# Two hybrid decoder layers on one core: values of two heads in one projection, the indexer's key beside the values, the rope key behind the first query tile, and another order of the sparse attention's first steps

## Chip, core and metric

The kernel runs on one core of a Trainium2 chip. The metric is the device time of one execution in microseconds; of several executions the median counts. The engines are PE (TensorE, matmuls), DVE (VectorE), ACT (ScalarE), POOL (GpSimd) and SP (SyncE, which issues most DMAs).

## What is computed

Two decoder layers over 512 tokens of 1024 features, in fp32. Each layer is a token mixer, a cross-attention into 256 memory tokens and a SwiGLU feed-forward part, each followed by a residual LayerNorm. The first mixer is multi-head latent attention (MLA), the second a sparse attention with an indexer (DSA). Cut to what the change touches:

```
# MLA: one input projection gives cq (512), ckv (256) and the rope key (32)
h = x @ w_in
q  = rms_norm(h[..., :512]) @ w_uq;  kv = rms_norm(h[..., 512:768]) @ w_ukv
k_rope = apply_rope(h[..., 768:800], pos)          # one key for all heads
# cross-attention, 4 heads of 256
q = x @ w_q;  k, v = split(mem @ w_kv)
p = softmax(q k^T / 16);  y = (p v) @ w_o
# DSA: queries 1024, keys 256, values 256, indexer queries 512, key 64, weights 8
h = x @ w_in
score = sum_h w_idx_h * relu(q_idx_h . k_idx / 8)   # top 128 keys of each query stay
p = softmax(q k^T / 8 + bias[bucket(distance)] on the chosen keys);  y = (p v) @ w_o
```

## The kernel before

Every product in full precision is three matmuls (`mm3`, L121, records on L122, L123, L124): operands are split into a high part, rounded by a cast on ACT (L99), and a low part, the difference, made by DVE or POOL (L101); high by high, high by low and low by high are accumulated in PSUM. Weights come in chunks of 512 KB (`chunk`, L108: load by SP, L112, then the split), through three `raw` buffers and five each for high and low parts. Activations lie transposed, features on partitions, in tiles of 2 KB (`t2`, 39 of them) and 8 KB (`t8`, 9) per partition. PSUM has two groups of four banks, "a" and "b". A framework puts the instructions on the engines in an order by priority and dependences, close to the order of the code; an engine then runs its own list strictly in order.

**The beginning** (L167 to L573). x comes transposed in three loads on SP's queue and is split in four pieces. The compression of keys and values with the rope key, 304 columns (`w_ckv`), is loaded in four chunks of two k-blocks: three on ACT's queue, the fourth on SP's (L491) when a buffer is free. 96 matmuls of 304 columns fill four banks. Positions and constants for the angles are loaded after that (L508, L509); DVE computes the angles (`trig`, L449). For each of four token tiles the rope key is copied four times side by side by two ACT copies (L521), transposed by PE (L522), and copied to SBUF (L524). Then come the four chunks of `w_cq` and four query tiles of 24 matmuls of 512 columns; each tile's normalising (`rms_t`, L527: square on ACT, L530; DVE, L533; transposes, L536) is placed behind a later tile's matmuls.

**Cross-attention** (`xa_kv` L714, `cross` L733). Per head: scores, the next head's queries, its keys (48 matmuls of 256 columns, memory tokens moving) and its values (48 of 256 columns, weights moving, two chunks), then the softmax's normalising, its transposes (L766), and the product with the values.

**DSA projections** (L930 to L971). Values and the eight indexer weights are one projection, 264 columns moving, token tiles as stationary operand: 96 matmuls. The indexer's key, twice 64 features, is a feature tile of its own (`w_ki`): 24 matmuls of 512 columns. Four tiles of indexer queries follow, and scores for the top-k.

**DSA attention** (L1004 to L1121). 16 items (query tile, group of four heads), item = 4 x tile + group. Eight projections of queries run in a loop, DVE doing five top-k steps in each (L978, L979); the high parts of the queries are made by ACT, low parts by POOL (`stack_q_pool`, L927, L928). Between them, and after, stand the steps of the items: `s` (scores, L1026 to L1028, then scaling with the bias on DVE, L420), `t` (normalising and transposes, L1041, L1043), `p` (product with the values, L1060, L1061, L1071, and output copies on POOL, L1076, L1077). The order is written out:

```
steps = {2: "s0", 3: "t0", 4: "s1 p0", 5: "t1", 6: "s2 p1", 7: "t2"}   # after query projection j
run_s(3); run("p2"); run_s(4); run_t(3)     # then, for i = 3 to 15: scores ahead, t of the next, p of i
```

The bias of an item is read from a table in DRAM (`dsa_bias`, L1004, DMA at L1008): those of the first four items early, into `t2` tiles, the others with the scores, into `t8` tiles.

## Time and profile before

| | us |
|---|---|
| median of three timed runs | 1540.42 |
| lowest, highest | 1538.08, 1541.06 |
| the profiled execution's own time | 1538.13 |
| its span, first to last instruction | 1536.3 |
| PE busy | 1503.6 (98%) |
| DVE, ACT, POOL busy | 994.9, 650.2, 303.9 |
| mean granted clock of PE | 0.996 |

A row of a timeline is one instruction, or some alike in a row. A matmul's record spans from its start to its modelled end and overlaps its successor's, so that the price of one is read from the distance of two starts. Brackets give the time in which the engine had nothing running, and what it waited for.

### The profile page before, as it was taken

How to read it: one execution, taken by the hardware profiler on the slowest of the kernel's cores; microseconds unless marked ns; L12 is line 12 of the kernel's file. 1: busy time of each engine (PE TensorE's matmuls, PEld its weight loads, DVE VectorE, ACT ScalarE, POOL GpSimd, SP SyncE). 2: the span in 40 equal slices, each digit the busy share in tenths (PEclk: the TensorE clock that was granted, in tenths of full speed). 3: DMA queues.
4: the chain of work that ended last, by engine and by line, in shares of the span. 5: the costliest groups of instructions: out<-in, count | busy, mean ns of one | idle time of the engine just before them, and what ended most of it. 6: DMA issues, size and time to landing. Idle time of an engine off the chain costs nothing.

```text
span 1536.3 us, 20733 instructions
## 1 busy us (share of the span) xinstructions
PE 1503.6 (98%) x7902; PEld 1283.5 (84%) x7902; DVE 994.9 (65%) x1741; ACT 650.2 (42%) x1158; POOL 303.9 (20%) x299
## 2 busy tenths in 40 slices
PE   8999999999999999999999989999999999999997
PEld 7788889988898888888888787898988888888886
DVE  7787868454746665654668988675448465656545
ACT  5677753343233333332246577344332433333230
POOL 1222001000032331400024653000002322324002
PEclk9999999999999999999999999999999999999999
DMA  6233424323333232233242147333323233222221
GB/s 214 71 98 107 155 83 134 125 85 97 124 97 101 77 124 97 96 97 108 84 138 87 51 158 240 110 119 102 110 94 125 83 110 98 102 94 90 97 96 55
DMA packets 51417, 166.45 MB, mean 108 GB/s; under 512 B 5300, under 2 KB 11972, under 8 KB 49268
## 3 DMA queue, kind: packets, MB, share of 16 engines
q1 hardware_dynamic: 50740, 164.18, 32.6%
q8 instruction: 62, 1.02, 0.3%
q10 hardware_dynamic: 576, 0.93, 0.2%
q14 instruction: 39, 0.32, 0.1%
HBM read 160.86 MB, written 9.47 MB: 111 GB/s over the span
## 4 chain that ended last, share of the span: by engine, by line
PE 88%; DVE 5%; ACT 3%; DMA 2%; issue 1%; POOL 1%; SPq 0%; POOLq 0%; DVEq 0%; ACTq 0%
PE ps L122 27%; PE ps L123 27%; PE ps L124 27%; DVE t L101 2%; PE ps L336 1%; ACT wh L99 1%; ACT t L426 1%; ACT t L99 1%; DMA raw<-in_w_cq_dram 1%; PE ps L1043 1%; PE ps L644 1%; DMA t<-in_xT_dram 1%; PE ps L1060 0%; POOL wl L101 0%; DMA t<-scr 0%
## 5 line engine op out<-in xcount | busy, mean ns | idle before, releaser
L122 PE MATMUL ps<-t,wh 128*128 128x512 f32 (+1 forms) x1256 | 456.2, 364 | 3.5 <-DVE t L101 3.4
L123 PE MATMUL ps<-t,wh 128*128 128x512 f32 (+1 forms) x1256 | 455.2, 362 | 0.8 <-DVE t L101 0.8
L124 PE MATMUL ps<-t,wl 128*128 128x512 f32 (+1 forms) x1256 | 454.9, 362 | 0.0
L99 ACT CAST wh<-raw 128x1024 fp32r<-128x1024 f32 (+3 forms) x219 | 227.4, 1038 | 450.0 <-PE ps L123 167.1
L101 DVE TENSOR_TENSOR wl<-raw,wh 128x1024 fp32r<-128x1024 f32 (+2 forms) x198 | 253.2, 1280 | 218.0 <-ACT wh L99 216.3
L122 PE MATMUL ps<-wh,t 128*128 128x512 f32 (+3 forms) x838 | 305.4, 364 | 1.1 <-ACT t L426 0.9
L123 PE MATMUL ps<-wl,t 128*128 128x512 f32 (+3 forms) x838 | 303.1, 362 | 1.2 <-DVE wl L101 1.2
L124 PE MATMUL ps<-wh,t 128*128 128x512 f32 (+3 forms) x838 | 303.0, 362 | 0.2 <-DVE t L101 0.2
L122 PEld LDWEIGHTS ps<-t,wh 128*128 128x128 f32 x1256 | 237.1, 189 | 41.5 <-DVE t L101 5.5
L123 PEld LDWEIGHTS ps<-t,wh 128*128 128x128 f32 x1256 | 237.2, 189 | 37.0 <-DVE t L101 1.3
L124 PEld LDWEIGHTS ps<-t,wl 128*128 128x128 f32 x1256 | 237.1, 189 | 36.6
L122 PEld LDWEIGHTS ps<-wh,t 128*128 128x128 f32 x838 | 158.5, 189 | 25.1 <-ACT t L426 1.3
L123 PEld LDWEIGHTS ps<-wl,t 128*128 128x128 f32 x838 | 158.4, 189 | 24.6 <-DVE wl L101 1.4
L124 PEld LDWEIGHTS ps<-wh,t 128*128 128x128 f32 x838 | 158.4, 189 | 24.0 <-DVE t L101 0.4
L99 ACT CAST t<-ps 128x512 fp32r<-128x512 f32 (+2 forms) x249 | 122.9, 525 | 129.3 <-PE ps L336 86.1
L279 POOL TENSOR_TENSOR sm<-sm,mhalf 128x1 f32<-128x1 f32 x32 | 28.6, 893 | 689.0 <-DVE sm L277 689.0
L101 DVE TENSOR_TENSOR t<-ps,t 128x512 fp32r<-128x512 f32 (+2 forms) x249 | 144.1, 607 | 20.3 <-ACT t L99 19.5
L99 ACT CAST wh<-t 128x1024 fp32r<-128x1024 f32 x56 | 58.9, 1052 | 141.9 <-PE ps L123 123.6
L101 DVE TENSOR_TENSOR wl<-t,wh 128x1024 fp32r<-128x1024 f32 x56 | 71.2, 1272 | 65.2 <-ACT wh L99 63.4
L863 DVE TENSOR_TENSOR t<-ps,t 128x512 f32<-128x512 f32 x44 | 30.4, 692 | 120.1 <-PE ps L124 120.1
L101 DVE TENSOR_TENSOR t<-t,t 128x512 fp32r<-128x512 f32 (+2 forms) x113 | 84.5, 751 | 23.0 <-ACT t L99 20.7
L99 ACT CAST t<-t 128x512 fp32r<-128x512 f32 (+2 forms) x113 | 64.5, 574 | 56.2 <-POOL t L797 33.6
(178 smaller groups left out, 1654.5 us busy)
## 6 DMA issues: line engine op xcount, KB each, us to landing
raw<-in_ffn_in_dram SPq DMA_DIRECT2D x88, 512.0 KB, 3.5
t<-in_ffn_dg_dram SPq DMA_DIRECT2D x16, 1024.0 KB, 5.0
raw<-in_xa_k_dram SPq DMA_DIRECT2D x16, 512.0 KB, 3.5
raw<-in_xa_v_dram SPq DMA_DIRECT2D x16, 512.0 KB, 3.9
raw<-in_xa_q_dram SPq DMA_DIRECT2D x16, 512.0 KB, 3.9
raw<-in_xa_o_dram SPq DMA_DIRECT2D x16, 512.0 KB, 3.4
raw<-in_ffn_dl_dram SPq DMA_DIRECT2D x12, 512.0 KB, 3.4
scr<-vscr SPq DMA_DIRECT2D x16, 319.5 KB, 4.4
```

The source lines that it names most:

```text
L99: nc.scalar.copy(h, src)
L101: (eng or nc.vector).tensor_tensor(l, src, h.bitcast(F32), op=ALU.subtract)
L122: nc.tensor.matmul(ps, st[0], mv[0], start=start, stop=False, skip_group_check=more)
L123: nc.tensor.matmul(ps, st[0], mv[1], start=False, stop=False, skip_group_check=more)
L124: nc.tensor.matmul(ps, st[1], mv[0], start=False, stop=stop, skip_group_check=more)
L279: nc.gpsimd.tensor_tensor(b, a, mhalf, op=ALU.pow)
L336: nc.tensor.transpose(pt[:, k], x_of(tt)[:, 512 * n + P * k:512 * n + P * k + P], ident)
L426: nc.scalar.activation(Sx, src, AF.Exp, bias=nb, scale=scale, accum_out=self.sm[:, i:i + 1])
L644: nc.tensor.transpose(pt[:, P * qt:P * qt + P], Ss[qt][:, P * kb:P * kb + P], ident)
L863: nc.vector.tensor_tensor(sg, pu, sg, op=ALU.mult)
L1043: nc.tensor.transpose(pt[:, P * i:P * i + P], Ss[i][:, P * kb:P * kb + P], ident)
```

## The change

Five edits.

1. `w_ckv` is laid out with all k-blocks side by side and loaded in three tiles of three, three and two k-blocks (first tile in two pieces, of one and two k-blocks), all on ACT's queue; there is no fourth load on SP. Positions and constants stand behind x at the head of SP's queue.
2. The copies, transposes and last copy of the rope key become `rope_key()`, called after the first query tile and the normalising of the first key/value tile.
3. The values of heads 0 and 1, and of 2 and 3, are projected together: 48 matmuls of 512 columns ahead of an even head, from four chunks, and none ahead of an odd one. The transposes of a head's softmax (`turned`) stand before the next head's keys.
4. `w_ki` is gone; its 64 columns are the last of `w_vi`, 328 columns wide. Per token tile ACT copies them twice side by side, and PE transposes them into one bank.
5. The scores of item 0 come after the fourth query projection and not the third, and so on; behind the last projection the scores of items 4, 3 and 5 come before the product of item 2. The bias of item 4 is read early too, into two `t2` tiles by two DMAs.

The diff, cut to its core (the host's layout functions, which follow it, are left out):

```diff
-    def pairs_of(tile_):
-        return tile_[:, 0:2 * NC0].rearrange("p (k m) -> p k m", k=2)
-    raw_w = [pairs_of(wp.tile([P, 1024], F32, tag="raw", name=nm("raw"), bufs=3)) for _ in range(3)]
+    def threes(tag, dt, bufs=5):
+        ts = [wp.tile([P, 1024], dt, tag=tag, name=nm(tag), bufs=bufs) for _ in range(3)]
+        return [t[:, 0:3 * NC0].rearrange("p (k m) -> p k m", k=3) for t in ts]
+    raw_w = threes("raw", F32, 3)
...
-    wr = A["w_ckv"].rearrange("c p (k m) -> c p k m", k=2)
-    for i in range(2):
+    wr = A["w_ckv"].rearrange("p (k m) -> p k m", k=NK)
+    for i, ks in enumerate((slice(0, 1), slice(1, 3))):
         nc.sync.dma_start(raw_x[0][:, i], xr[0, :, i])
-        nc.scalar.dma_start(raw_w[0][:, i], wr[0, :, i])
+        nc.scalar.dma_start(raw_w[0][:, ks], wr[:, ks])
...
+    posi = t2(I32)
+    nc.sync.dma_start(posi, A["positions"].broadcast_to((P, S)))
+    nc.sync.dma_start(cst, A["consts"])
...
+    w_parts = {0: (0, 0, 1), 1: (0, 1, 3), 2: (1, 0, 3), 6: (2, 0, 2)}
...
-            sw = slice(i, i + step)
-            split(wh[:, sw], wl[:, sw], rw[:, sw])
+            if 2 * c + i in w_parts:
+                t, a, b = w_parts[2 * c + i]
+                split(whs[t][:, a:b], wls[t][:, a:b], raw_w[t][:, a:b])
...
-    pkb = bank("a")
-    for tt in range(NT):
-        kr = t2(F32, (P, 2, 2, 32))
-        for a in range(2):
-            c0 = 256 + 16 * a
-            nc.scalar.copy(kr[:, a], ps2[tt][:, c0:c0 + 32].unsqueeze(1).broadcast_to((P, 2, 32)))
-        nc.tensor.transpose(pkb[:, ts_of(tt)], kr.rearrange("p a b c -> p (a b c)"), ident)
     pk = t2()
-    nc.scalar.copy(pk, pkb)
+    def rope_key():
+        pkb = bank("a")
+        for tt in range(NT):
...
+        nc.scalar.copy(pk, pkb)
...
         rms_t(ps2[tt], 256, tt, gkv[:, 0:256], ckv)
         if tt:
             rms_t(psq[tt - 1], 512, tt - 1, gq, cq)
+        if tt == 0:
+            rope_key()
...
-        ws = [chunk(A["xa_v"][i, hd, c], (P, 4, 256)) for c in range(2)]
-        pv = bank("a", (P, 2, 256))
-        for mt in range(2):
-            for k in range(NK):
+        if hd % 2:
+            return Kt, None
+        ws = [chunk(A["xa_v"][i, hd // 2, c], (P, 2, 512)) for c in range(4)]
+        pvs = [bank("a") for _ in range(2)]
+        for k in range(NK):
+            w = ws[k // 2]
+            for mt in range(2):
                 ms = slice(P * mt, P * mt + P)
-                w = ws[k // 4]
-                mm3(pv[:, mt], (m[k][0][:, ms], m[k][1][:, ms]), (w[0][:, k % 4], w[1][:, k % 4]), k == 0, k == NK - 1)
+                mm3(pvs[mt], (m[k][0][:, ms], m[k][1][:, ms]), (w[0][:, k % 2], w[1][:, k % 2]), k == 0, k == NK - 1)
...
             Ss = scores(hd, Q)
             if hd < 3:
                 Q = q_proj(hd + 1)
+            PT = turned(Ss)
+            if hd < 3:
                 kvs[hd + 1] = xa_kv(i, hd + 1, m)
-            pv(hd, Ss)
+            pv(hd, PT)
...
+    pk = bank("b")
...
-            mm3(pv[:, 0:264], (xh[:, ts_], xl[:, ts_]), (w[0][:, k % 3], w[1][:, k % 3]), k == 0, k == NK - 1)
+            mm3(pv[:, 0:NV], (xh[:, ts_], xl[:, ts_]), (w[0][:, k % 3], w[1][:, k % 3]), k == 0, k == NK - 1)
...
-    (pk,) = proj_tiles([chunk(A["w_ki"], (P, NK, P))], XT, False)
+        ki = t2(F32, (P, 2, 64))
+        nc.scalar.copy(ki, pv[:, 264:NV].unsqueeze(1).broadcast_to((P, 2, 64)))
+        nc.tensor.transpose(pk[:, ts_], ki.rearrange("p a b -> p (a b)"), ident)
...
-        bt = t8(F32, (P, 4, 512)) if qt else t2(F32, (P, 4, P))
-        read = nc.sync.dma_start(bt[:, :, 0:n],
+        if (qt, g) == (1, 0):
+            bts = [t2(F32, (P, 2, 256)) for _ in range(2)]
+        else:
+            bts = [t8(F32, (P, 4, 512)) if qt else t2(F32, (P, 4, P))]
...
-        bt = dsa_bias(qt, g) if qt else first_bias[g]
+        bt = dsa_bias(qt, g) if 4 * qt + g > 4 else first_bias[4 * qt + g]
...
-    steps = {2: "s0", 3: "t0", 4: "s1 p0", 5: "t1", 6: "s2 p1", 7: "t2"}
+    steps = {3: "s0", 4: "t0 s1", 5: "p0 t1", 6: "s2 p1", 7: "t2"}
...
-        if j < 4:
-            first_bias.append(dsa_bias(0, j))
+        if j < 5:
+            first_bias.append(dsa_bias(j // 4, j % 4))
...
+    run_s(4)
     run_s(3)
+    run_s(5)
     run("p2")
-    run_s(4)
     run_t(3)
     for i in range(3, 16):
         a = 1 if i < LA else 0
         if i != LA:
-            run_s(i + 1 + a)
+            if i > 3:
+                run_s(i + 1 + a)
             run_t(i + a)
```

How it moves instructions, at two places. In the names, `ps` is a PSUM bank and the numbers tell buffers apart; the diff shifts line numbers (L99 becomes L100, L122 to L124 become L123 to L125, L522 becomes L528, L536 becomes L540, L1026 to L1028 become L1051 to L1053).

**The rope key, on ACT.** Before, from the third `w_cq` cast on: four-fold copies of the key (L521), the `w_v` cast, the copy back (L524), the first square (L530):

```order
L99 CAST wh_312<-raw_310 128x1024
L99 CAST wh_318<-raw_316 128x1024
L521 COPY t_37_280<-ps_127 128x64 x2
L521 COPY t_38_284<-ps_128 128x64 x2
L521 COPY t_39_288<-ps_129 128x64 x2
L521 COPY t_40_292<-ps_130 128x64 x2
L99 CAST wh_541<-raw_539 128x1024
L524 COPY t_41_296<-ps_279 128x512
L530 ACTIVATE t_55_347,sm_348<-ps_127 128x256
```

After:

```order
L100 CAST wh_288<-raw_286 128x1024
L100 CAST wh_294<-raw_292 128x1024
L534 ACTIVATE t_47_323,sm_324<-ps_130 128x256
L100 CAST wh_535<-raw_533 128x1024
L527 COPY t_54_338<-ps_130 128x64 x2
L527 COPY t_55_342<-ps_131 128x64 x2
L527 COPY t_56_346<-ps_132 128x64 x2
L527 COPY t_57_350<-ps_133 128x64 x2
L100 CAST t_12_122<-ps_332 128x2x128
L529 COPY t_33_273<-ps_337 128x512
```

The square of the first key/value tile (L534) and the `w_v` cast now stand ahead of the copies (L527), and the copies behind all four `w_cq` casts as before.

**The same place on PE.** Before: the last 304-column matmul, the transposes of the rope key (L522) among the first matmuls of the first query tile (`ps_322`), its end, and the first normalising's transposes (L536):

```order
L124 MATMUL ps_130<-wh_227,t_10_118 128x304
L522 MATMUL ps_279<-ident,t_37_280 128x128
L522 MATMUL ps_279<-ident,t_38_284 128x128
L522 MATMUL ps_279<-ident,t_39_288 128x128
L122 MATMUL ps_322<-wh_300,t_7_115 128x512
L522 MATMUL ps_279<-ident,t_40_292 128x128
L123 MATMUL ps_322<-wl_301,t_7_115 128x512
L124 MATMUL ps_322<-wh_300,t_8_116 128x512
...
L124 MATMUL ps_322<-wh_318,t_10_118 128x512
L536 MATMUL ps_356<-ident,t_59_354 128x128 x2
L122 MATMUL ps_367<-wh_300,t_7_115 128x512
```

After:

```order
L125 MATMUL ps_133<-wh_136,t_11_121 128x304
L123 MATMUL ps_298<-wh_276,t_8_118 128x512
L124 MATMUL ps_298<-wl_277,t_8_118 128x512
L125 MATMUL ps_298<-wh_276,t_9_119 128x512
...
L125 MATMUL ps_298<-wh_294,t_11_121 128x512
L540 MATMUL ps_332<-ident,t_51_330 128x128 x2
L528 MATMUL ps_337<-ident,t_54_338 128x128
L528 MATMUL ps_337<-ident,t_55_342 128x128
L528 MATMUL ps_337<-ident,t_56_346 128x128
L528 MATMUL ps_337<-ident,t_57_350 128x128
L123 MATMUL ps_361<-wh_276,t_8_118 128x512
```

The whole first query tile (`ps_298`) follows the last 304-column matmul; the transposes of the first key/value tile (L540) and of the rope key (L528) stand between it and the second tile.

**The end of the query projections, on PE.** Before: the last matmul of the eighth projection (`ps_11530`), item 2's transposes (L1041), item 3's scores (four pairs L1027, L1028; the last two use the last projection's queries) with item 2's remainder (L105, which subtracts the high part) among them:

```order
L124 MATMUL ps_11530<-t_1393_10106,wl_11527 128x512
L1041 MATMUL ps_11567<-ident,t_1578_11099 128x128 x4
L1027 MATMUL ps_11579<-t_1554_10981,t_1667_11459 128x256
L1028 MATMUL ps_11579<-t_1554_10981,t_1667_11459 128x256
L1027 MATMUL ps_11584<-t_1554_10981,t_1668_11460 128x256
L1028 MATMUL ps_11584<-t_1554_10981,t_1668_11460 128x256
L1027 MATMUL ps_11589<-t_1554_10981,t_1693_11555 128x256
L1028 MATMUL ps_11589<-t_1554_10981,t_1693_11555 128x256
L105 MATMUL ps_11567<-t_1699_11572,identn 128x512
L1027 MATMUL ps_11594<-t_1554_10981,t_1694_11556 128x256
```

After (L1051 adds the mask, so the groups of three are item 4's scores; item 3's pairs follow on `ps_11489` and `ps_11494`):

```order
L125 MATMUL ps_11414<-t_1390_10004,wl_11411 128x512
L1066 MATMUL ps_11451<-ident,t_1576_10979 128x128 x4
L1051 MATMUL ps_11463<-t_1538_10777,identr 128x256
L1052 MATMUL ps_11463<-t_1545_10815,t_1553_10870 128x256
L1053 MATMUL ps_11463<-t_1545_10815,t_1553_10870 128x256
...
L1051 MATMUL ps_11481<-t_1538_10777,identr 128x256
L1052 MATMUL ps_11481<-t_1545_10815,t_1553_10870 128x256
L106 MATMUL ps_11451<-t_1699_11456,identn 128x512
L1053 MATMUL ps_11481<-t_1545_10815,t_1553_10870 128x256
L1052 MATMUL ps_11489<-t_1552_10861,t_1667_11343 128x256
L1053 MATMUL ps_11489<-t_1552_10861,t_1667_11343 128x256
L1052 MATMUL ps_11494<-t_1552_10861,t_1668_11344 128x256
```

Item 4's twelve matmuls stand between item 2's transposes and item 3's scores.

## Rows read from the trace of the kernel before

**Rows 1.** The page's head, the first line of its part 1 and the line of engines of its part 4 (the chain that ended last). Part 1 gives busy us, share of the span and number of instructions.

```profile
span 1536.3 us, 20733 instructions
...
PE 1503.6 (98%) x7902; PEld 1283.5 (84%) x7902; DVE 994.9 (65%) x1741; ACT 650.2 (42%) x1158; POOL 303.9 (20%) x299
...
PE 88%; DVE 5%; ACT 3%; DMA 2%; issue 1%; POOL 1%; SPq 0%; POOLq 0%; DVEq 0%; ACTq 0%
```

**Rows 2.** The list of waits of PE over the whole span: what waited, for whom, us in total, number of times, longest us.

```profile
PE ps L522 <- ACT t L521: 3.6, 1, 3.6
...
PE ps L1027 <- POOL t L927: 3.2, 2, 2.8
...
PE ps L1026 <- DVE sm L420: 1.3, 1, 1.3
```

**Rows 3.** PE's timeline, four pairs of neighbours' first and last at full clock: values of a head (256 columns), indexer key and the queries after it (512), values (264), key/value compression (304). Columns: start in us, us, engine, line, operation, out<-in, shape, count.

```profile
263.20 0.28 PE L122 MATMUL ps<-wh,t 128*128 128x256 f32 x1
...
264.17 0.28 PE L124 MATMUL ps<-wh,t 128*128 128x256 f32 x1
...
786.06 0.39 PE L122 MATMUL ps<-t,wh 128*128 128x512 f32 x1
...
790.82 0.39 PE L122 MATMUL ps<-t,wh 128*128 128x512 f32 x1
...
782.18 0.28 PE L122 MATMUL ps<-wh,t 128*128 128x264 f32 x1
...
783.87 0.29 PE L124 MATMUL ps<-wh,t 128*128 128x264 f32 x1
...
20.20 0.30 PE L123 MATMUL ps<-wl,t 128*128 128x304 f32 x1
...
20.89 0.30 PE L122 MATMUL ps<-wh,t 128*128 128x304 f32 x1
```

**Rows 4.** The table of five stretches: us from and to, length, then for PE, PEld, DVE, ACT, POOL the busy us and (number of instructions), mean granted clock, DMA share, GB/s. 205 to 330 lies in the first cross-attention, 765 to 825 are values, indexer key and indexer queries, 855 to 895 the end of the sparse attention's query projections and what follows.

```profile
25.00:30.00 5.00, 4.90 (x16) 3.82 (x17) 4.83 (x8) 2.90 (x13) 0.00 (x0) 0.66 0.51 181
205.00:330.00 125.00, 124.94 (x779) 112.32 (x777) 76.91 (x125) 46.28 (x76) 4.63 (x7) 1.00 0.37 118
765.00:825.00 60.00, 59.97 (x325) 50.58 (x324) 39.44 (x70) 31.05 (x54) 14.52 (x8) 1.00 0.37 123
855.00:885.00 30.00, 29.40 (x146) 24.22 (x145) 28.94 (x83) 16.21 (x37) 15.98 (x16) 1.00 0.08 25
885.00:895.00 10.00, 7.02 (x42) 6.03 (x41) 7.92 (x28) 6.00 (x17) 4.30 (x7) 0.83 0.38 129
```

**Rows 5.** PE's timeline at the beginning; in brackets idle us before, and the releaser.

```profile
11.37 0.41 PE L123 MATMUL ps<-wl,t 128*128 128x304 f32 x1 [1.22 <-DVE wl L101]
...
21.17 0.30 PE L124 MATMUL ps<-wh,t 128*128 128x304 f32 x1
25.10 0.79 PE L522 MATMUL ps<-ident,t 128*128 128x128 f32 x3 [3.63 <-ACT t L521]
...
29.46 0.42 PE L122 MATMUL ps<-wh,t 128*128 128x512 f32 x1
...
38.89 0.81 PE L536 MATMUL ps<-ident,t 128*128 128x128 f32 x6
39.46 0.48 PE L122 MATMUL ps<-wh,t 128*128 128x512 f32 x1
```

**Rows 6.** ACT's timeline around the copies of the rope key.

```profile
23.77 1.04 ACT L99 CAST wh<-raw 128x1024 fp32r<-128x1024 f32 x1 [1.19 <-DMA raw<-in_w_cq_dram]
24.73 1.01 ACT L521 COPY t<-ps 128x64 f32<-128x64 f32 x8
```

**Rows 7.** DVE's timeline at the beginning: the low part of the third and fourth k-blocks' weights, that of the fourth query-compression chunk, and the normalising of the first query tile.

```profile
10.53 0.78 DVE L101 TENSOR_TENSOR wl<-raw,wh 128x608 fp32r<-128x608 f32 x1
...
26.28 1.22 DVE L101 TENSOR_TENSOR wl<-raw,wh 128x1024 fp32r<-128x1024 f32 x1
...
35.51 0.75 DVE L533 SCALAR_TENSOR_TENSOR t<-ps,sm,t 128x512 f32<-128x512 f32 x1 [0.66 <-POOL sm L279]
```

**Rows 8.** PE's timeline in the sparse attention: scores of item 0, then the end of the last query projection and the scores of item 3.

```profile
849.54 0.39 PE L1027 MATMUL ps<-t,t 128*128 128x256 f32 x1 [0.47 <-POOL t L927]
...
850.88 0.39 PE L1027 MATMUL ps<-t,t 128*128 128x256 f32 x1 [0.84 <-POOL t L928]
...
885.24 1.05 PE L1041 MATMUL ps<-ident,t 128*128 128x128 f32 x8
...
889.53 0.49 PE L1027 MATMUL ps<-t,t 128*128 128x256 f32 x1 [2.77 <-POOL t L927]
...
892.17 0.56 PE L1026 MATMUL ps<-t,identr 128*128 128x256 f32 x1
```

**Rows 9.** POOL's timeline ahead of the scores of item 3.

```profile
888.22 1.26 POOL L927 TENSOR_TENSOR t<-t,t 64x512 fp32r<-64x512 f32 x1
```

**Rows 10.** DVE's timeline around it, and its wait for a bias later.

```profile
885.67 0.40 DVE L1072 TENSOR_TENSOR t<-t,ps 128x256 f32<-128x256 f32 x1
...
888.90 0.27 DVE L420 CUSTOM_DVE_ANT_0 t<-ps,t 128x128 f32<-128x128 f32 x1
...
932.87 0.69 DVE L420 CUSTOM_DVE_ANT_0 t<-ps,t 128x512 f32<-128x512 f32 x1 [1.59 <-DMA t<-scr]
```

**Rows 11.** Part 6 of the page: DMA issues, count, KB each, median us from issue to landing.

```profile
raw<-in_xa_v_dram SPq DMA_DIRECT2D x16, 512.0 KB, 3.9
```

More of the change, by code (lines that the diff above doesn't have):

```diff
@@ L38 @@
 WARM = 8
+NV = 256 + 8 + 64
 NC0 = 256 + 32 + 16
@@ L515, in tile_hybrid_mla_dsa_deepnorm_block @@
     nc.sync.dma_start(gkv[:, 0:256], A["kv_norm"].broadcast_to((P, 256)))
-    pkb = bank("a")
-    for tt in range(NT):
-        kr = t2(F32, (P, 2, 2, 32))
-        for a in range(2):
-            c0 = 256 + 16 * a
-            nc.scalar.copy(kr[:, a], ps2[tt][:, c0:c0 + 32].unsqueeze(1).broadcast_to((P, 2, 32)))
-        nc.tensor.transpose(pkb[:, ts_of(tt)], kr.rearrange("p a b c -> p (a b c)"), ident)
     pk = t2()
-    nc.scalar.copy(pk, pkb)
     wcq = [chunk(A["w_cq"][c], (P, 2, 512)) for c in range(4)]
+    def rope_key():
+        pkb = bank("a")
+        for tt in range(NT):
+            kr = t2(F32, (P, 2, 2, 32))
+            for a in range(2):
+                c0 = 256 + 16 * a
+                nc.scalar.copy(kr[:, a], ps2[tt][:, c0:c0 + 32].unsqueeze(1).broadcast_to((P, 2, 32)))
+            nc.tensor.transpose(pkb[:, ts_of(tt)], kr.rearrange("p a b c -> p (a b c)"), ident)
+        nc.scalar.copy(pk, pkb)
     def rms_t(ps, n, tt, g, dst):
@@ L757, in scores, with turned @@
             return sx
-        def pv(hd, sx):
+        def turned(sx):
             Ss = sx.normalise()
-            Vt = kvs[hd][1]
             PT = []
@@ L928, in stack_q_pool @@
         nc.gpsimd.tensor_tensor(QB[0:64], f[64:128], QB[64:128].bitcast(F32), op=ALU.subtract)
-    wvs = [chunk(A["w_vi"][:, 264 * k0:264 * k1], (P, k1 - k0, 264)) for k0, k1 in ((0, 3), (3, 6), (6, 8))]
+    wvs = [chunk(A["w_vi"][:, NV * k0:NV * k1], (P, k1 - k0, NV)) for k0, k1 in ((0, 3), (3, 6), (6, 8))]
     VD = t8(FR, (P, 4, 4, P))
+    pk = bank("b")
     wi = cp.tile([P, NT, 8], F32, name="wi")
@@ L1006, in dsa_bias @@
         c0 = 127 + 384 - 128 * qt
-        bt = t8(F32, (P, 4, 512)) if qt else t2(F32, (P, 4, P))
-        read = nc.sync.dma_start(bt[:, :, 0:n],
-                                 scr[bass.ds(r * (1 + qt), 1), 4 * g:4 * g + 4, :, c0:c0 + n].rearrange("a h p k -> p (a h) k"))
+        if (qt, g) == (1, 0):
+            bts = [t2(F32, (P, 2, 256)) for _ in range(2)]
+        else:
+            bts = [t8(F32, (P, 4, 512)) if qt else t2(F32, (P, 4, P))]
+        m = 4 // len(bts)
+        for i, bt in enumerate(bts):
+            read = nc.sync.dma_start(bt[:, :, 0:n],
+                                     scr[bass.ds(r * (1 + qt), 1), 4 * g + m * i:4 * g + m * i + m, :,
+                                         c0:c0 + n].rearrange("a h p k -> p (a h) k"))
         reads.append(read)
-        return bt
+        return [bts[i // m][:, i % m, 0:n] for i in range(4)]
     Q, OTd = [], {}
@@ L1020, in dsa_scores @@
         ts_ = slice(P * qt, P * qt + P)
-        bt = dsa_bias(qt, g) if qt else first_bias[g]
-        sx = Softmax([bt[:, i, 0:n] for i in range(4)])
+        bt = dsa_bias(qt, g) if 4 * qt + g > 4 else first_bias[4 * qt + g]
+        sx = Softmax(bt)
         for i in range(4):
@@ L1196, in layout @@
     f["xa_k"] = np.stack([_fm(I["xa_w_kv"][i][:, :1024]) for i in range(2)])
-    f["xa_v"] = np.stack([_tm(I["xa_w_kv"][i][:, 1024:], 4, 256) for i in range(2)])
+    f["xa_v"] = np.stack([_tm(I["xa_w_kv"][i][:, 1024:], 2, 512) for i in range(2)])
     f["xa_o"] = np.stack([_tm(I["xa_w_o"][i], 2, 512) for i in range(2)])
```

40 lines of the change are left out of this document (20 added, 20 removed).

## The prediction, made before the changed kernel ran

> **What bounds the kernel.** I read the page's totals first, then PE's list of waits, then timelines of the two places where PE waits longest, then a table of stretches. PE is busy 1503.6 of 1536.3 us and holds 88% of the chain that ended last [rows 1]: nearly everywhere a microsecond less of PE's work is a microsecond less of span, and work moved on another engine counts only where PE waits for it. The waits of PE are few. The longest is the 3.6 us of L522 for ACT's L521, the copies of the rope key; next come L1027 for POOL's L927, 3.2 us, and L1026 for DVE's L420, 1.3 us [rows 2]. So three things have to be costed: matmuls whose number and width change (stages that are 100% PE), the beginning, and the sparse attention's steps. The stretches that count for the first are full: 124.94 of 125 us in a cross-attention, 59.97 of 60 where values, indexer key and indexer queries are projected [rows 4].
>
> **Prices of a matmul.** Taken as starts of neighbours at full clock, not as the records' own durations, which overlap [rows 3]. 256 columns: 263.20 to 264.17 is 8 intervals, 0.121 each. 512: 786.06 to 790.82 is 21, 0.227. 264: 782.18 to 783.87 is 14, 0.121. 304: 20.20 to 20.89 is 5, 0.138. A 128-column transpose: six from 38.89 to 39.46, 0.095 [rows 5].
>
> **Values of two heads together.** Per layer 4 heads x 2 blocks x 8 k x 3 = 192 matmuls of 256 columns become 96 of 512. Both layers: 384 x 0.121 = 46.5 us becomes 192 x 0.227 = 43.6: **-2.9**. The medians over all such records in the trace (0.120 and 0.2275) give -2.4; I take **-2.5**. It all lies on PE's path, since the stretch has no idle. Loads, casts and subtracts are as many as before (16 chunks of 512 KB), but four now stand ahead of an even head and none of an odd one. The transposes of the scores move ahead of the next head's keys; they are the same eight instructions. What that may cost is a rival below.
>
> **Indexer key beside the values.** Gone: 24 matmuls x 0.227 = 5.45, one chunk. Added: 64 columns on 96 matmuls. No row shows 328 columns: below it is 304 at 0.138, above it 512 at 0.227, and on the line between them 0.148. So 96 x (0.148 - 0.121) = 2.6; the bounds are 96 x 0.017 = 1.6 and 96 x 0.106 = 10.2, and I take the line because 264 to 304 already climbs by the same slope. Four transposes at 0.095 to 0.11 add 0.4. Their copies are on ACT, beside PE's next block; the last one's copy stands alone before the key's split, but the projections of the indexer queries follow on PE and cover it. Sum **-2.4** (bounds -3.5 and +5).
>
> **The beginning.** Three pieces. (a) PE's 1.22 us at 11.37 waits for the low part of the third k-block's weights, written by DVE at 10.53, behind the low part of x [rows 5, 7]. With k-blocks 1 and 2 split in one instruction that low part comes first, and the next late thing is x's own: **-0.8** (0 to -1.2). (b) The rope key. PE has its last 304-column matmul at 21.17 and its next instruction at 25.10, 3.63 us idle [rows 5]. ACT ran the copies only at 24.73, since the fourth query-compression chunk's cast at 23.77, itself waiting for its DMA, is ahead of them [rows 6]. Then PE is at the lower clock, mean 0.66 of full in 25 to 30 [rows 4]: from 25.10 to 29.46 stand nine matmuls and four transposes, 9 x 0.227 + 4 x 0.1 = 2.4 us of work in 4.36, so 1.9 more is lost. Together 5.5. The change lets the 24 matmuls of the first query tile run straight after 21.17, and puts the copies and transposes behind it. Not all comes back: those matmuls need the fourth chunk's low part, which DVE starts at 26.28 [rows 7] because the chunk came late, and which takes 1.2; six matmuls of the tile need it, so the tile ends near 28.6 where PE alone would end it at 25.9. Then come the transposes of the first normalised key/value tile; its square now stands behind the rope copies on ACT and then ahead of them, so I take them to be ready at about that time. And the transposes of the first query tile wait for L533 at 35.51 to 36.26 [rows 7], at the end of a stretch in which DVE is full (4.83 of 5 us in 25 to 30 [rows 4]). That chain moves little, so the third query tile, at 39.46 now, starts at about 36.9 [rows 5]. That is **-2.5** for (a) and (b) together; bounds 0 (all turned into those later waits) and -6.7 (5.5 + 1.2, all gone). (c) The positions and constants at the head of the queue cost two issues of 0.4 us on SP, hidden behind the loads of x that were issued before them.
>
> **The sparse attention's steps.** The scores of item 0 move from the third to the fourth query projection. They now wait 0.47 at 849.54 and 0.84 at 850.88, for POOL's low parts of the queries [rows 8]; one projection later these are long done: -1.3 there. Yet this stage is also paced by DVE, busy 28.94 of 30 us in 855 to 885 [rows 4], so I keep half, **-0.6**. At the end, item 3 needs the last queries: PE's last projection is through at 885.24, its next useful step waits 2.77 us for POOL until 889.53, and PE then runs at the lower clock to 892.17 [rows 8] (mean 0.83 in 885 to 895 [rows 4]): eight instructions, 4 x 0.121 + 2 x 0.227 + 2 x 0.1 = 1.1 us of work, take 2.6, so the place costs 2.8 + 1.5 = 4.3 in all. POOL reaches L927 at 888.22 because its output copies for item 1 wait for DVE's L1072 at 885.67, among the top-k steps [rows 9, 10]. The change puts item 4, which needs no late queries, in front: 12 matmuls x 0.121 = 1.45 us of useful work in the hole. But items 3 and 4 share four banks: item 3 now waits until DVE has taken item 4's scores, and DVE works through top-k steps first: today from L1072 at 885.67 to its first scores at 888.90 [rows 10], after the change with one such step more, so to about 889.5. So the hole shrinks by 1.45 and no more: **-1.4**. The bias tiles loaded one item ahead could take the 1.3 us of L1026, where DVE waits 1.59 us for a bias that is being read [rows 2, 10], if its buffer were free sooner; I take nothing for it. Together **-2.0**; bounds +2 (the bank wait outlasts today's and the clock stays low longer) and -6.9 (1.3 + 4.3 + 1.3).
>
> **Sum.** -2.5 - 2.4 - 2.5 - 2.0 = -9.4 against the profiled execution's 1538.13 us: 1528.7. That execution is close to the lowest of the three timed ones and 2.3 under their median; a median lies 0 to 3 above such a run, so I add 1 and forecast **1530**.
>
> **A rule that speaks against it.** The rows give 2 x 0.121 for two narrow matmuls and 0.227 for the wide one, 15 ns in favour of pairing [rows 3]. The Trainium skill, page "TensorE: Matmul & The Clock Gate", section Back-to-back issue gap, gives an isolated matmul's spacing as its columns over 2.4 GHz plus 2.5 ns. By that, pairing would be worth 192 x 2.5 ns, an estimate of 0.5 us, and the sum two microseconds less; in this trace both widths cost more than that, the narrow one more so.
>
> **Rivals.**
> 1. *The waits go altogether* (rope 5.5 + 1.2, and 6.9 in the sparse attention): -4.9 - 6.7 - 6.9 = -18.5, so 1521. For it: the waiting instructions really leave the places. Against: in both places DVE is full, so another wait is next. Chance 0.13.
> 2. *The waits come back one for one* and only the matmul counts remain: -4.9, so 1534. For it: DVE's 4.83 of 5 us in 25 to 30 and 28.94 of 30 in 855 to 885 [rows 4]. Chance 0.17.
> 3. *A matmul costs its columns and nothing else*, so that pairing brings nothing where the trace's 15 ns stem from the order of operands and not the width: -6.9, so 1532. The rows speak against it at all three widths between 256 and 512. This is the mechanism of the page's rule. Chance 0.04.
> 4. *Slower: chunks arrive too late in the even heads.* Keys and values of an even head now need six chunks in 48 x 0.121 + 48 x 0.227 = 16.7 us instead of four in 96 x 0.121 = 11.6, with three raw buffers and 3.9 us from issue to landing [rows 11]. Should PE wait one landing in each of the four such stages, +15.6 - 9.4 = 1545. It decides from (9.4 + 3) / 4 = 3.1 us lost per stage. Against: 16.7 / 6 = 2.8 us per chunk is hardly less than today's 2.9, and DVE has 48 us spare in the 125 [rows 4]. Chance 0.05.
> 5. *It does not do what it says*: the freed time of values and beginning is given back because DVE paces the sparse attention, and only the cross-attention's -2.5 remains: 1535.6 + 1 = 1537, hardly to be told from no change. Chance 0.06.
>
> **Chances.** Forecast (1526 to 1533) 0.55. About 0.2%, 3 us, can be told from no change. Faster: 0.55 + 0.13 + 0.04 + most of rival 2 = 0.87; same 0.08; slower 0.05. The range takes in rivals 1 and 2 and the median's spread: 1521 to 1537.
>
> **What will show it.** Right: PE goes from the last 304-column matmul into the query tile with no idle time of over 1 us; the third query tile starting near 37; 328-column matmuls 0.148 apart; 512-column value matmuls 0.227 apart with PE full in the cross-attention; item 3's wait named DVE or POOL and shorter by over 1 us. Wrong: a wait for a raw buffer or a DMA inside the keys and values of even heads, 328 columns nearer 0.2, or transposes of the rope key that still stop PE for 3 us, behind the first query tile.

## The result

| | before | changed |
|---|---|---|
| median of six runs, us | 1538.93 | 1530.09 |
| lowest, highest | 1537.51, 1541.06 | 1528.05, 1530.63 |
| ratio, 95% interval | | 0.994 [0.9927, 0.9952] |
| the profiled execution, its span | 1538.13, 1536.3 | 1530.63, 1528.8 |

The changed kernel is 8.8 us faster by the medians, and 7.5 by the two profiled executions: of before a low one was profiled, of the changed kernel the highest. Run once more beside the experiments, it had 0.9938 [0.9925, 0.9952].

The page's head, the line of busy times and that of the chain, after (before: [rows 1]):

```profile
span 1528.8 us, 20325 instructions
...
PE 1497.2 (98%) x7690; PEld 1269.8 (83%) x7690; DVE 994.6 (65%) x1739; ACT 651.2 (43%) x1160; POOL 303.6 (20%) x299
...
PE 84%; DVE 9%; ACT 2%; issue 2%; DMA 2%; POOL 0%; POOLq 0%; SPq 0%; DVEq 0%; ACTq 0%
```

PE's busy time fell by 6.4 us and its share is the same: what went is mostly PE's work. PE's list of waits after (before: [rows 2]; the columns are the same):

```profile
PE ps L106 <- ACT t L105: 3.7, 3, 3.3
...
PE ps L124 <- DVE wl L102: 1.9, 1, 1.9
...
PE ps L341 <- DVE t L337: 1.0, 2, 0.8
PE ps L540 <- ACT t L527: 1.0, 1, 1.0
...
PE ps L540 <- DVE t L537: 0.9, 1, 0.9
```

The wait for the copies of the rope key and that for POOL ahead of item 3 are gone. In their place stand 3.3 us of L106 (the remainder of an item's transposes, L105 before) for ACT, 1.9 us for the low part of a query chunk, and 0.8 to 1.0 us at three transposes. Three stretches (columns as in [rows 4]):

```profile
25.00:30.00 5.00, 2.23 (x12) 1.53 (x12) 4.52 (x9) 1.19 (x9) 0.71 (x1) 1.00 0.32 108
205.00:330.00 125.00, 125.00 (x714) 109.72 (x714) 79.20 (x127) 47.00 (x73) 3.96 (x4) 1.00 0.39 120
855.00:885.00 30.00, 25.76 (x130) 21.20 (x129) 27.63 (x78) 14.92 (x36) 14.28 (x19) 0.94 0.07 20
```

In 25 to 30 the clock is 1.00 where it was 0.66, so the beginning got better. In 855 to 885 it is 0.94 where it was 1.00, and PE's busy time there is 25.76 where it was 29.40. But the changed kernel runs some 5.4 us ahead there (its last score matmul of the indexer starts at 818.71, that of before at 824.16), so the stretch to compare with is this one of before:

```profile
860.45:890.45 30.00, 26.93 (x136) 22.26 (x134) 28.87 (x84) 16.04 (x40) 17.05 (x20) 0.99 0.16 53
```

So in the sparse attention's query projections and what follows them PE is busy 1.2 us less, not 3.6.

To see where the time went, I read in each trace the starts of PE's transposes that every kernel has, and took the distances:

| stretch, by PE's instructions | before | changed | alone |
|---|---|---|---|
| start to the first softmax transposes of MLA | 70.43 | 68.16 | edits 1 and 2: 67.40; edit 2: 66.98 |
| first cross-attention: last transposes of the norm ahead of it to the first of the norm behind it | 143.17 | 140.80 | edit 3: 140.78; its order alone: 141.81 |
| that norm, first to last transposes | 22.37 | 23.27 | 23.31; 23.04 |
| second cross-attention, likewise | 143.41 | 140.77 | 140.73; 142.03 |
| first transposes of the norm behind layer 0's feed-forward part to the indexer's first scores | 37.83 | 35.96 | edit 4: 35.98 |
| the indexer's last scores to the norm behind the sparse attention | 173.74 | 173.67 | edit 5: 175.60 |

The first, the third and the last row are not steady: in five kernels with the old beginning the first row reads 69.5 to 70.5 (mean 70.0), in eight with the new one 66.8 to 68.2 (mean 67.5). The norm in the third row reads 22.4 to 22.8 in five kernels with the cross-attention of before (mean 22.5) and 22.4 to 23.3 in eight with edit 3 (mean 23.0). The last reads 171.6 to 174.3 in seven kernels without edit 5 (mean 172.9), and 172.7, 173.7 and 175.6 in the three with it. So the beginning is worth 2.5, the two cross-attentions 2.4 and 2.6 less the 0.5 that the norm takes back in the mean, the key 1.9, and edit 5 nothing or a loss.

### The profile page after: what moved, and what is told of

Same layout as the page of the kernel before. It is cut to its first block, busy times and chain, and to the rows that moved or that the text cites. A ratio compares the mean times of both kernels' runs of the same rounds, so it can differ in the third digit from the quotient of the medians.

```text
span 1528.8 us, 20325 instructions
## 1 busy us (share of the span) xinstructions
PE 1497.2 (98%) x7690; PEld 1269.8 (83%) x7690; DVE 994.6 (65%) x1739; ACT 651.2 (43%) x1160; POOL 303.6 (20%) x299
## 4 chain that ended last, share of the span: by engine, by line
PE 84%; DVE 9%; ACT 2%; issue 2%; DMA 2%; POOL 0%; POOLq 0%; SPq 0%; DVEq 0%; ACTq 0%
PE ps L124 26%; PE ps L123 26%; PE ps L125 26%; DVE t L102 2%; DVE t L998 1%; DVE m L997 1%; ACT t L431 1%; PE ps L341 1%; DVE wl L102 1%; PE ps L1068 1%; DMA raw<-in_w_cq_dram 1%; ACT wh L100 1%; PE ps L650 1%; DMA raw<-in_ffn_in_dram 1%; PE ps L1086 1%
## 5 line engine op out<-in xcount | busy, mean ns | idle before, releaser
L123 PE MATMUL ps<-t,wh 128*128 128x512 f32 (+1 forms) x1248 | 454.0, 364 | 4.2 <-DVE t L102 3.4
L124 PE MATMUL ps<-t,wh 128*128 128x512 f32 (+1 forms) x1248 | 452.7, 363 | 0.8 <-DVE t L102 0.8
L125 PE MATMUL ps<-t,wl 128*128 128x512 f32 (+1 forms) x1248 | 452.3, 362 | 0.0
L100 ACT CAST wh<-raw 128x1024 fp32r<-128x1024 f32 (+2 forms) x217 | 226.6, 1044 | 438.0 <-PE ps L124 158.7
L123 PE MATMUL ps<-wh,t 128*128 128x512 f32 (+3 forms) x774 | 294.7, 381 | 0.1
L124 PE MATMUL ps<-wl,t 128*128 128x512 f32 (+3 forms) x774 | 292.3, 378 | 2.0 <-DVE wl L102 1.9
L125 PE MATMUL ps<-wh,t 128*128 128x512 f32 (+3 forms) x774 | 292.1, 377 | 0.3 <-DVE t L102 0.3
L123 PEld LDWEIGHTS ps<-t,wh 128*128 128x128 f32 x1248 | 235.9, 189 | 42.0 <-DVE t L102 5.5
L124 PEld LDWEIGHTS ps<-t,wh 128*128 128x128 f32 x1248 | 235.9, 189 | 36.8 <-DVE t L102 1.2
L125 PEld LDWEIGHTS ps<-t,wl 128*128 128x128 f32 x1248 | 235.9, 189 | 36.4
L100 ACT CAST t<-ps 128x512 fp32r<-128x512 f32 (+2 forms) x249 | 122.4, 526 | 117.8 <-PE ps L341 86.5
L124 PEld LDWEIGHTS ps<-wl,t 128*128 128x128 f32 x774 | 145.5, 188 | 28.0 <-DVE wl L102 2.8
L123 PEld LDWEIGHTS ps<-wh,t 128*128 128x128 f32 x774 | 145.7, 188 | 26.1 <-DVE t L102 0.4
L125 PEld LDWEIGHTS ps<-wh,t 128*128 128x128 f32 x774 | 145.4, 188 | 26.4 <-DVE t L102 0.6
L100 ACT CAST wh<-t 128x1024 fp32r<-128x1024 f32 x56 | 58.9, 1052 | 141.5 <-PE ps L124 123.5
L100 ACT CAST t<-t 128x512 fp32r<-128x512 f32 (+2 forms) x113 | 64.6, 575 | 57.0 <-POOL t L813 33.6
```

What stands on the lines that cost most here:

```text
L100: nc.scalar.copy(h, src)
L123: nc.tensor.matmul(ps, st[0], mv[0], start=start, stop=False, skip_group_check=more)
L124: nc.tensor.matmul(ps, st[0], mv[1], start=False, stop=False, skip_group_check=more)
L125: nc.tensor.matmul(ps, st[1], mv[0], start=False, stop=stop, skip_group_check=more)
```

## The experiments

Ratios are to the kernel before on the same chip, with 95% intervals; 0.001 is 1.5 us.

**Edit 3 alone.** The kernel before with the diff's lines in `xa_kv` and `cross`.

> The kernel before with edit 3 alone (values of two heads projected together, transposes of the softmax ahead of the next head's keys). Theory A: the two cross-attentions hold two gains, 1.2 us each from 96 matmuls of 512 columns in place of 192 of 256, and some 1.2 us each from small waits (about 0.2 us at three places and 0.6 at one per layer) that go because the transposes are earlier; about 1 us comes back where the norm behind the cross-attention waits for DVE. Total -3.5 us. Theory B: only the matmul counts pay, -2.4 us. Theory C, from the rival with late chunks: slower, with a wait for a DMA or a split inside the keys and values of even heads.

Measured: 0.9961 [0.9948, 0.9974], -6.0 us, more than theory A's -3.5. In the trace the cross-attentions are 2.4 and 2.7 us shorter and the norm behind the first one gives 0.9 back: theory A's parts, at -4.1 in all. The ratio's interval reaches down to -4.0; the beginning and the sparse attention of this run happened to be 0.6 and 1.2 us shorter as well, without a change in them. No wait for a chunk in the even heads: the rival with late chunks is out.

**Its order alone.** Values per head as before; only

```diff
                 Q = q_proj(hd + 1)
+            PT = turned(Ss)
+            if hd < 3:
                 kvs[hd + 1] = xa_kv(i, hd + 1, m)
-            pv(hd, Ss)
+            pv(hd, PT)
```

> The kernel before with only the order inside the cross-attention changed: the transposes of a head's softmax stand before the next head's keys and values; the values stay one head at a time, 256 columns. Theory A: the small waits go, -2.4 us in both layers together, less what the norm behind gives back (up to 1 us). Theory B: the same instructions in another order, 0 within 0.5 us.

Measured: 0.9981 [0.9972, 0.999], -2.9 us; 1.4 us less in each cross-attention, 0.7 back in the norm. Theory A. So of what edit 3 gives in these stretches, somewhat more than half is the moved transposes (2.7 us, of which the norm takes 0.7 back here), and the wider matmuls give the rest, 1.0 us in the first layer and 1.3 in the second. One of the places, PE's timeline at the last head of the first layer, before:

```profile
366.39 0.28 PE L124 MATMUL ps<-t,t 128*128 128x256 f32 x1
367.10 0.50 PE L122 MATMUL ps<-wh,t 128*128 128x512 f32 x1 [0.43 <-ACT t L426]
```

and with the order alone:

```profile
366.88 0.40 PE L124 MATMUL ps<-wh,t 128*128 128x512 f32 x1
367.13 1.14 PE L765 MATMUL ps<-ident,t 128*128 128x128 f32 x8
```

In both kernels nine matmuls of the output projection stand between the last head's scores and its transposes. Before, the first of them waits for ACT's exponentials of these scores, which start only at 366.48, behind the casts for the product of the head before; with the order alone the exponentials start at 364.30, the nine run without a wait, and the transposes follow at 367.13. Part of the time that is won ends in a norm that is not ready (this row is of the changed kernel, at the norm behind the first cross-attention):

```profile
421.43 0.63 PE L341 MATMUL ps<-ident,t 128*128 128x128 f32 x4 [0.83 <-DVE t L337]
```

**Edit 4 alone.** The lines with `NV`, `ki` and `w_vi`.

> The kernel before with edit 4 alone (indexer's key beside the values, 328 columns, and no feature tile of its own). Theory A: -2 us at the first scores of the indexer, and the same at the end. Theory B: the sparse attention behind it is paced by DVE, so the 2 us are there at the indexer's first scores, and are given back by the product of the last item; end 0.

Measured: 0.9989 [0.998, 0.9997], -1.7 us, and 1.85 in its stretch, still there at the end (-2.4). Theory A.

**Edits 1 and 2 alone.**

> The kernel before with edits 1 and 2 alone (layout and loads of the key/value compression, positions early, rope key behind the first query tile). Theory A: -2.3 us at the first softmax transposes of the first layer, as in the trace of the changed kernel, kept to the end. Theory B: kept only up to the sparse attention, which DVE paces, and given back there; end 0.

Measured: 0.9977 [0.9966, 0.9987], -3.5 us; 3.0 at the first softmax transposes, against a mean of 70.0 rather 2.6, and 2.6 at the end. Theory A. That the gain comes through the sparse attention also says that not everything ahead of it is given back there.

**Edit 2 alone.** The move of `rope_key()` without the new layout.

> The kernel before with edit 2 alone (rope key behind the first query tile; the key/value compression is laid out and loaded as before). By the prediction's split: of the 3.1 us that edits 1 and 2 gave together at the first softmax transposes, 0.8 is the layout's, so -2.3 is left; the new wait, for the low part of the fourth query chunk, is over 1.9 us here, since that chunk is loaded as late as before. Rival: the chunk's load is what counts, and without edit 1 the wait takes back nearly all: -0.5.

Measured: 0.9982 [0.9973, 0.9991], -2.8 us. Its first softmax transposes start at 66.98, no later than with edit 1 as well (67.40). PE's waits in this kernel (L539 is the normalising's transposes):

```profile
26.33 0.50 PE L123 MATMUL ps<-wl,t 128*128 128x512 f32 x1 [0.39 <-DVE wl L101]
...
28.48 0.44 PE L539 MATMUL ps<-ident,t 128*128 128x128 f32 x2 [0.72 <-ACT t L526]
```

The wait for the fourth query chunk is 0.39, not over 1.9 as the expectation had it; in the changed kernel it is 1.90 (below). The two traces are not alike, though. Up to 10.2 us PE ran at the lower of its two clock levels here, with 304-column matmuls 0.253 us apart (seven intervals between these rows; 0.138 in [rows 3]):

```profile
8.18 0.46 PE L123 MATMUL ps<-wl,t 128*128 128x304 f32 x1
...
9.95 0.46 PE L124 MATMUL ps<-wh,t 128*128 128x304 f32 x1
```

So it did not wait at the third k-block even with the old layout, and it came to the first query tile only at 21.46 (20.37 in the changed kernel), when the fourth chunk was nearly ready. Of the eight kernels with edits 1 and 2, four also ran at the lower level until 10 to 11 us: they wait under 0.2 us for that chunk, and their first softmax transposes start at 66.8 to 67.4. The other four were at the upper level by 7.1 us, wait 1.16 to 1.90 us for it, and start them at 67.4 to 68.2. Compared with its like, edit 2 alone loses nothing without edit 1. What the layout is worth where the upper level comes early is not shown: edit 2 alone has no such trace, and edit 1 alone was not run.

**Edit 5 alone.** The table of steps, the tail, the early bias.

> The kernel before with edit 5 alone (steps of the sparse attention, early bias of item 4, new tail). Theory A: what it takes away (1.6 us at item 0's scores, some 3 us of the hole ahead of item 3) comes back as a wait inside the query projections: item 2's first two scores now stand before item 1's remainder matmul, their scaling on DVE stands behind top-k steps, ACT's exponentials of item 2 stand ahead of the high part of item 1's transposes, and PE waits 3.3 us for that and runs at half clock behind it. Net 0 within 1 us. Theory B: DVE paces the whole stretch, so the order does not matter at all: also 0, but then with the lost time spread, and no single wait over 2 us ahead of the last projection. Theory C, the prediction's step: -2 us.

Measured: 1.0 [0.9991, 1.0008]; its stretch is 175.60 us. The wait is the one that theory A names; from the list of waits:

```profile
PE ps L105 <- ACT t L104: 3.7, 3, 3.3
```

The prediction's -2 is out.

**The changed kernel without edit 5.**

> The changed kernel with edit 5 undone (edits 1 to 4 stay). Theory A: as fast as the changed kernel within 1 us, about 1530, with item 3's wait of 2.8 us back and none at item 1's remainder. Theory C: 2 us slower than the changed kernel.

Measured: 0.9933 [0.992, 0.9945], against 0.994 and 0.9938 of the changed kernel. Not slower without edit 5; whether it is 1 us faster these intervals don't tell. It is 10.3 us faster than the kernel before, and edit 3, edit 4 and edits 1 and 2, each measured alone, add up to 11.2: within the intervals the edits do not disturb each other. PE's longest waits in it are those of before:

```profile
843.34 0.39 PE L1046 MATMUL ps<-t,t 128*128 128x256 f32 x1 [0.51 <-POOL t L943]
...
883.35 0.48 PE L1046 MATMUL ps<-t,t 128*128 128x256 f32 x1 [2.77 <-POOL t L943]
```

**Two other tables of steps in the changed kernel.** First `{2: "s0", 3: "t0", 4: "s1 p0", 5: "t1", 6: "s2 p1", 7: "t2"}` as before, with the new tail:

> The changed kernel with only the table of steps inside the query projections as before (item 0 after the third, and so on); the tail with items 4, 3, 5 in front and the early bias stay. In the built order item 2's scores then stand behind item 1's remainder again. Theory A: the wait of 3.3 us and the half clock behind it go (-5.8), item 0's waits (+1.6) and two small ones (+0.5) come back: 3 to 4 us faster than the changed kernel. Theory B (DVE paces it): the same time as the changed kernel within 1 us, the waits turn up elsewhere before the tail.

Then `{3: "s0", 4: "t0", 5: "s1 p0", 6: "t1", 7: "s2 p1"}` and a tail of items 4, 2's transposes, 3, 5:

> The changed kernel with the steps one projection later: item 0 after the fourth, its transposes after the fifth, item 1's scores and item 0's product after the sixth, item 1's transposes after the seventh, item 2's scores and item 1's product after the eighth, then items 4, 2's transposes, 3, 5. Neither item 0's scores nor item 1's remainder has to wait in the built order. Theory A: 4 to 6 us faster than the changed kernel, unless the tail, which now holds item 2 as well, waits longer for DVE's top-k. Theory B (DVE paces it): the same time as the changed kernel within 1 us.

Measured: 0.993 [0.9918, 0.9943] and 0.993 [0.9917, 0.9943]; stretches of 171.50 and 171.36 us. Theory A's 3 to 6 us over the changed kernel are not there (1.2 to 2.3 in the trace, 1.2 to 1.5 by ratio), and theory B's "the same" is not excluded. PE's waits, first kernel (the last of these rows is item 3):

```profile
842.50 0.39 PE L1052 MATMUL ps<-t,t 128*128 128x256 f32 x1 [0.51 <-POOL t L943]
...
882.42 0.35 PE L1052 MATMUL ps<-t,t 128*128 128x256 f32 x1 [1.01 <-DVE sm L425]
```

second kernel:

```profile
857.50 0.50 PE L106 MATMUL ps<-t,identn 128*128 128x512 f32 x1 [0.30 <-ACT t L105]
...
871.36 0.47 PE L123 MATMUL ps<-t,wh 128*128 128x512 f32 x1 [1.95 <-DVE t L1093]
...
880.78 0.39 PE L1051 MATMUL ps<-t,identr 128*128 128x256 f32 x1 [1.87 <-DVE sm L425]
...
885.15 0.36 PE L1052 MATMUL ps<-t,t 128*128 128x256 f32 x1 [0.75 <-DVE sm L425]
```

The 3.3 us are gone in both, and item 3's wait falls from 2.77 to 1.01 and 0.75. But in the second kernel 1.95 and 1.87 us for DVE appear at places that had none. I added up, from the starts of PE's neighbours, what every gap of over 0.13 us beyond the price of its matmul loses between the indexer and the norm: 12.6 us before and 10.3 without edit 5 (one and the same order), 12.5 and 11.4 in two runs of the changed kernel, 10.1 and 10.2 here. Orders that differ in nearly every step lose what the old order loses, within its own spread.

**Half of the top-k.** In the changed kernel

```diff
         for it in its:
+            if it % 2 == 0:
+                continue
```

> The changed kernel with every second top-k step left out (8 of 16 per query tile, so only half as many keys are struck from the list; some 24 x 1.4 = 34 us less for DVE, nothing less for PE). The order on PE keeps item 2's first scores ahead of item 1's remainder. Theory B (DVE paces the stretch): the waits of PE from the first scores to the last product, 12.5 us in the changed kernel, fall to under 4, and the kernel is some 9 us faster than the changed one. Theory A in its strict form (the order alone makes the wait): the 3.3 us at item 1's remainder stay.

and the same without edit 5:

> The changed kernel without edit 5 and with every second top-k step left out, as in the run beside it. Theory B: the waits, 10.3 us with all top-k steps, fall to under 4, and the time equals that of the run beside it within 1 us, since the order stops to matter once DVE has room. Theory A: it stays 2 us ahead of the run beside it.

Every second top-k step is left out, so that 64 keys of a query are chosen where the kernel chooses 128. Measured: 0.9912 [0.9897, 0.9927] and 0.992 [0.9905, 0.9935]; stretches of 166.83 and 168.91 us, where the two kernels have 173.67 (172.69 when run again) and 171.57 with all steps. Two waits of PE with edit 5, of 0.23 us at item 0's remainder and 0.48 ahead of the seventh projection, are all over 0.2 us up to item 2's remainder:

```profile
857.44 0.50 PE L106 MATMUL ps<-t,identn 128*128 128x512 f32 x1 [0.23 <-ACT t L105]
...
864.79 0.50 PE L123 MATMUL ps<-t,wh 128*128 128x512 f32 x1 [0.48 <-ACT t L942]
```

The wait of 3.3 us is gone though item 2's first scores still stand ahead of item 1's remainder on PE (the remainder itself is four matmuls earlier): DVE's top-k steps made it. Theory A in its strict form is out. But theory B's numbers miss too: the gaps still lose 6.0 and 7.8 us, not under 4, and the kernel is 4 us faster than the changed one, not 9. With DVE relieved, edit 5's stretch is 2.1 us shorter than the old order's, which would be the -2.0 of the prediction; with all steps it is no shorter. That the order matters once DVE has room is not shown by this: it is one trace each, traces of the old order with all steps differ by 2.7 us, and the ratios' intervals overlap. DVE's busy time in the stretch (third figure with a count in each row) without edit 5, all steps:

```profile
818.00:989.00 171.00, 164.53 (x871) 137.77 (x870) 148.94 (x415) 109.94 (x253) 69.86 (x94) 0.99 0.41 138
```

and half of the steps:

```profile
818.00:986.00 168.00, 162.97 (x870) 136.38 (x869) 122.22 (x342) 109.60 (x253) 69.31 (x94) 1.00 0.41 139
```

26.7 us less of DVE gives 2.7 us of the stretch.

**The changed kernel again.**

> The changed kernel once more, beside the others on one chip. Against the kernel without edit 5 (0.9933 of the kernel before, in an earlier comparison): if edit 5 costs the 2.1 us by which its stretch is longer in the two traces, 0.9946; if it costs nothing, 0.9933.

Measured: 0.9938 [0.9925, 0.9952]; it lies between the two values, and the intervals are wider than their distance. What edit 5 is worth in time, between a gain of 1.4 us (the interval of edit 5 alone) and a loss of 2 (the stretches), stays open.

## Why the prediction was right, and where it was not

The forecast of 1530 met 1530.09, but two of its four terms were off by about 2 us each, in opposite ways, so that the meeting to 0.1 us is luck. Between the two profiled executions the change is -7.5 us, where the terms add up to -9.4.

*The beginning: right, -2.5 against -2.5.* PE's timeline after (columns as in [rows 5]):

```profile
10.54 0.41 PE L125 MATMUL ps<-wh,t 128*128 128x304 f32 x1 [0.31 <-DVE t L102]
...
20.23 0.30 PE L125 MATMUL ps<-wh,t 128*128 128x304 f32 x1
20.37 0.40 PE L123 MATMUL ps<-wh,t 128*128 128x512 f32 x1
...
26.79 0.50 PE L124 MATMUL ps<-wl,t 128*128 128x512 f32 x1 [1.90 <-DVE wl L102]
...
29.20 0.44 PE L540 MATMUL ps<-ident,t 128*128 128x128 f32 x2 [0.99 <-ACT t L527]
...
36.82 0.66 PE L540 MATMUL ps<-ident,t 128*128 128x128 f32 x4 [0.91 <-DVE t L537]
37.23 0.47 PE L123 MATMUL ps<-wh,t 128*128 128x512 f32 x1
```

PE goes from the last 304-column matmul, 20.23, into the query tile at 20.37. Then come the waits that the step named: 1.90 for the fourth chunk's low part, 0.99 at the first normalised tile, 0.91 at the first query tile's transposes, and the third tile starts at 37.23 (forecast 36.9, before 39.46). The rope transposes no longer stop PE. Two things are less firm than the sum. The split: the wait at the third k-block did fall from 1.22 to 0.31, but edit 2 alone gives as much as both, in a trace in which PE started at the lower level and had no such wait to lose. And the waits: the changed kernel run again, also at the lower level at first, has none for the fourth chunk, 0.39 and 0.89 us at the two transposes, and its third tile starts at 35.91.

*The prices: right.* From 258.74 to 262.38 are 16 intervals of 512 columns, 0.2275 each; from 778.06 to 778.96 are 6 of 328, 0.150 (forecast 0.148):

```profile
258.74 0.40 PE L125 MATMUL ps<-wh,t 128*128 128x512 f32 x1
...
262.38 0.39 PE L123 MATMUL ps<-wh,t 128*128 128x512 f32 x1
...
778.06 0.31 PE L125 MATMUL ps<-wh,t 128*128 128x328 f32 x1
...
778.96 0.32 PE L125 MATMUL ps<-wh,t 128*128 128x328 f32 x1
```

The key's -1.9 against -2.4 has 0.2 of its difference here (96 x 0.002); the other 0.3 was not measured by itself. Of the wide value matmuls, 2.3 in both layers was measured against 2.5. By the formula of the Trainium skill for an isolated matmul (page "TensorE: Matmul & The Clock Gate", section Back-to-back issue gap) pairing is worth an estimated 0.5. The measured 2.3 disagrees with that.

*The values: the step that failed is "the same eight instructions".* Moving the transposes was priced at nothing because the count is the same and the stretch is 99.95% busy in the table. But between neighbours' starts PE lost 1.2 us per layer there, three times 0.21 and once 0.59 (the row at 367.10 above is the last), and the move takes them. A matmul's record runs past its successor's start, so that such gaps hardly show as idle time. It gave 2.7 us, of which 0.7 came back at the norm in the run with the order alone.

*The sparse attention: the step that failed is "-1.4" and "-0.6".* At the end of the projections the forecast holds: item 4's scores fill the hole, and item 3 follows without a wait of its own (the 0.22 is item 2's remainder):

```profile
884.11 0.36 PE L1051 MATMUL ps<-t,identr 128*128 128x256 f32 x1
...
885.88 0.50 PE L106 MATMUL ps<-t,identn 128*128 128x512 f32 x1 [0.22 <-ACT t L105]
...
886.34 0.28 PE L1052 MATMUL ps<-t,t 128*128 128x256 f32 x1
```

The prediction even feared too much there, since item 3 does not wait for banks. What it left out stands a projection earlier. PE:

```profile
864.43 0.36 PE L1052 MATMUL ps<-t,t 128*128 128x256 f32 x1
...
865.89 0.50 PE L123 MATMUL ps<-t,wh 128*128 128x512 f32 x1 [0.74 <-ACT t L942]
...
873.54 0.79 PE L106 MATMUL ps<-t,identn 128*128 128x512 f32 x1 [3.27 <-ACT t L105]
...
876.65 0.28 PE L1052 MATMUL ps<-t,t 128*128 128x256 f32 x1
```

Item 2's first two scores (L1052, from 864.43) now stand ahead of item 1's remainder (L106). ACT, between them:

```profile
869.77 0.40 ACT L431 ACTIVATE t<-t,sm 128x128 f32<-128x128 f32 x1 [3.32 <-DVE sm L425]
...
872.38 0.40 ACT L431 ACTIVATE t<-t,sm 128x128 f32<-128x128 f32 x1 [2.12 <-DVE sm L425]
...
872.90 0.59 ACT L105 CAST t<-ps 128x512 fp32r<-128x512 f32 x1
```

and DVE:

```profile
869.45 0.28 DVE L425 CUSTOM_DVE_ANT_0 t<-ps,t 128x128 f32<-128x128 f32 x1
...
871.12 0.69 DVE L998 MATCH_REPLACE8 t<-m,t 128x512 f32<-128x512 f32 x1
871.73 0.41 DVE L1097 TENSOR_TENSOR t<-t,ps 128x256 f32<-128x256 f32 x1
872.05 0.28 DVE L425 CUSTOM_DVE_ANT_0 t<-ps,t 128x128 f32<-128x128 f32 x1
```

DVE takes those two scores only at 869.45 and 872.05, behind top-k steps (L997, L998) and item 0's output; ACT's exponentials (L431) wait for them, 3.32 and 2.12 us; the high part of item 1's transposes (L105, 872.90) is behind the exponentials on ACT, although the transposes that it reads stand on PE right ahead of 864.43; and PE waits 3.27 us for it and takes 3.11 us for seven matmuls worth 1.6. That is 3.3 + 1.5 = 4.8 us, most of the 1.3 + 4.3 that items 0 and 3 had cost. The order of ACT's instructions tells it; the prediction followed PE's there, and only behind the last projection. With half of DVE's top-k steps the wait is gone, so it is DVE's lateness that this order passes on to PE.

*The rivals.* The late chunks, with the slower ending, did not come: cross-attention is 125.00 of 125 us busy. "It does not do what it says", that the sparse attention gives back what is won ahead of it, is out: the gains of the key and of the beginning, each measured alone, are there at the end. "Waits come back one for one" holds for the sparse attention and not for the beginning, and "the waits go altogether" for neither. That a matmul costs its columns and nothing else is out by the 2.3 us of pairing.

*A row passed over.* The list of waits also has 3.4 us, in four waits, of L122 for DVE's L101, more than the 3.2 us that the prediction calls next. No edit was aimed at them, and they are still 3.4 us after.

## What to carry to other kernels

Count the distance of starts, not idle time, before calling a stretch full: an order that lets the next independent matmuls stand between a softmax and its product was worth as much here as half as many matmuls of twice the width (2.7 us less what the norm took back, against 2.3). Where a second engine is some 87% busy beside PE (148.94 of 171 us here), a change of order moved PE's waits, and their sum by no more than traces of one order differ; read every in-order queue between the moved step and the next consumer, since one early instruction can hold back a later one that was ready. And a sum that comes out to 0.1 us can still hide two errors of 2 us: only the edits one by one showed them. And before two traces are compared wait by wait, see that PE ran at the same level up to that place: here the same beginning had a wait of 1.90 us in one trace and none in another.
